# Feature sums in place on VectorE, the embedding's products behind the early pairs, and the gated embedding joined to the residual early

## The chip, the cores and the metric

The kernel runs on one core of a Trainium2 chip. It is one launch of some 43,600 instructions over five engines: TensorE (PE in the rows: matmuls, and PEld for its weight loads), VectorE (DVE), ScalarE (ACT), GpSimd (POOL) and SyncE (SP), which only issues DMAs. The metric is the device time in microseconds (us). Each engine runs its own list of instructions in the order in which the program laid it down, and waits on semaphores for the others.

## The reference

Two transformer-like blocks on a sequence of 1024 tokens with 1024 features. The change lies at the end of the second block, after its four branches have been merged:

```python
h = _layer_norm(DEEPNORM_ALPHA * h + merged @ w_out[i], ln1_g[i], ln1_b[i])
ffn = jnp.square(jax.nn.relu(h @ mlp_w1[i])) @ mlp_w2[i]
ple = jax.nn.sigmoid(h @ ple_gate_w[i]) * (p[i] @ ple_w[i])
h = _layer_norm(DEEPNORM_ALPHA * h + ffn + ple, ln2_g[i], ln2_b[i])
```

`mlp_w1` is 1024 x 4096, `mlp_w2` 4096 x 1024, `ple_gate_w` 1024 x 1024 and `ple_w` 256 x 1024. `p` is an input of 1024 x 256. All are fp32.

## The kernel before, in words

Activations lie transposed: 8 tiles of 128 features by 1024 tokens, in two chunks of 512 tokens. Each fp32 operand is split into a high part (a cast on ScalarE, L130 or L152) and a low part (a subtraction on VectorE, L131, or on GpSimd, L154), and a product is three matmuls: high by high, low by high, high by low (`mm3`, L160 to L162).

**The end of the second block** has these stages. The out-projection (`wo2`) makes one chunk of `h` after the other into 8 tiles `hs` (names `r` in the rows); a generator, `layer_norm`, is stepped between the matmuls and normalizes one chunk while the next is projected. Its sums over features are GpSimd additions (L2323), then one small matmul group for the mean (L2292), a spread of it by transposes (L2298), squares on ScalarE (L2333) that are added on GpSimd and VectorE in turn (L2335), a second pair L2292 and L2298, and the scaling (L2346, L2347). `done` splits the finished tiles into `hx`. Then come the embedding `p @ ple_w` (L2030 to L2053; 96 matmuls; result `wd`, "embedding", in DRAM), the products with `mlp_w1` and `ple_gate_w`, and the products with `mlp_w2`.

**The class `Seven`.** `h @ w` for a pair of 128-column groups of weights and the two chunks of tokens is a 2 x 2 block product. It is made with seven block products in place of eight (Winograd's form). A block product is 4 tiles x 3 = 12 matmuls of 512 columns. The features' sums t1 to t4 (differences of quarters of `h`) are made once, by `differences`; the weights' sums s1 to s4 are made per pair on GpSimd by `prepare` (L2204 to L2212), split, and consumed by `run`. There are 20 pairs: 16 of `mlp_w1` (`squared`), 4 of `ple_gate` (`gated`). The first two products of a pair, w11 y11 and w12 y21, need only plain quarters of `h` from the first chunk; for the first four pairs (EARLY) they are made ahead of the others, by `first`, while the second chunk is still being normalized. The `finish` functions square or gate a result and store it to DRAM. The gated result ("gated") and `h` itself ("normed") are read back ahead of the `mlp_w2` stage and joined to the residual.

**What sets the order.** The Tile framework places the instructions on the engines' lists by the order in the code and by when buffers come free, and adds the waits. Buffers come from rings of one SBUF pool: 29 slots, 11 temps, 6 weight buffers (`w`), 2 side buffers for loads (`l`), and 8 PSUM banks. SP issues nearly all DMAs from one list, in order: a DMA that waits for its data or its buffer holds up all DMAs behind it.

## Time and profile before

| what | us |
|---|---|
| three runs: lowest, median, highest | 3174.11, 3179.6, 3182.74 |
| the profiled execution, device time | 3182.6 |
| its span in the profile | 3180.8 |
| TensorE busy in it | 3038.2 |
| VectorE, ScalarE, GpSimd busy in it | 1785.6, 1151.4, 648.9 |

Times in the rows are us from the span's start. In a row of the timeline stand start, duration, engine, line, operation, output<-inputs, shape and count, and in brackets how long the engine was idle before it and what released it. The matmuls overlap, so a matmul's own duration (0.39) is longer than the distance to the next one's start (0.23). The out-projection of the second chunk ends at 2314, the embedding stands from there to 2353, the early pairs to 2379, the runs of the 20 pairs from 2404 to 2780, and the `mlp_w2` stage from there to the end.

### The profile page before, as it was taken

The numbers are of one execution on the slowest core, as the hardware profiler recorded it, in microseconds if no ns is written. First come the engines' busy times: TensorE is split into PE (matmuls) and PEld (weight loads), VectorE is DVE, ScalarE is ACT, GpSimd is POOL, SyncE is SP. The second block draws the span as 40 slices with busy tenths as digits, with TensorE's granted clock in tenths as the row PEclk, the third lists the DMA queues.
The fourth block names the chain that finished last, engine by engine and source line by source line (L and its number), as shares of the span: only waits on it lengthen the run. The fifth ranks groups of instructions, "written<-read, shape, count | busy, mean of one in ns | idle before, by whom it ended". The sixth has DMA issues, their size and how long they took to land.

```text
span 3180.8 us, 43621 instructions
## 1 busy us (share of the span) xinstructions
PE 3038.2 (96%) x17300; PEld 2647.7 (83%) x17300; DVE 1785.6 (56%) x3207; ACT 1151.4 (36%) x2192; POOL 648.9 (20%) x377
## 2 busy tenths in 40 slices
PE   8999999999999999999999998899977999989998
PEld 7999999999999778878877787687755888868887
DVE  4626777562567555354374647746657777652324
ACT  4224663222456442232245545512342222321113
POOL 1222001122200321010001000036624333212211
PEclk9999999999999999999999999999998999999999
DMA  3210004322000411111221010354242333562311
GB/s 119 81 65 25 16 21 165 113 68 83 27 11 27 152 63 57 57 49 54 86 94 67 34 40 30 105 184 140 92 178 83 119 111 109 194 225 91 96 60 54
DMA packets 111196, 273.94 MB, mean 86 GB/s; under 512 B 21372, under 2 KB 28540, under 8 KB 110992
## 3 DMA queue, kind: packets, MB, share of 16 engines
q1 hardware_dynamic: 109504, 266.52, 24.5%
q0 software_dynamic: 1488, 4.64, 0.6%
q8 instruction: 136, 2.23, 0.3%
q14 instruction: 68, 0.56, 0.1%
HBM read 202.79 MB, written 68.32 MB: 85 GB/s over the span
## 4 chain that ended last, share of the span: by engine, by line
PE 81%; DVE 8%; ACT 5%; DMA 2%; issue 2%; POOL 1%; SPq 0%; ACTq 0%; DVEq 0%; POOLq 0%
PE pj L160 13%; PE pj L162 13%; PE pj L161 13%; PE z L162 4%; PE z L161 4%; PE z L160 4%; PE fg L160 3%; PE fg L162 3%; PE fg L161 3%; PE pt L595 2%; PE x L1353 1%; PE sc L160 1%; PE sc L161 1%; PE sc L162 1%; PE sc L554 1%
## 5 line engine op out<-in xcount | busy, mean ns | idle before, releaser
L160 PE MATMUL pj<-hh,wih 128*128 128x348 f32 x864 | 278.8, 328 | 10.0 <-ACT wih L152 6.3
L161 PE MATMUL pj<-hl,wih 128*128 128x348 f32 x864 | 281.4, 326 | 3.4 <-DVE hl L690 3.2
L162 PE MATMUL pj<-hh,wil 128*128 128x348 f32 x864 | 280.0, 325 | 1.4 <-POOL wil L154 1.4
L160 PE MATMUL pj<-gh,m2h 128*128 128x512 f32 (+1 forms) x560 | 211.6, 378 | 12.3 <-ACT m2h L152 12.3
L160 PE MATMUL fg<-xx,fw 128*128 128x512 f32 x512 | 215.3, 421 | 0.0
L162 PE MATMUL pj<-gh,m2l 128*128 128x512 f32 (+1 forms) x560 | 210.4, 376 | 0.5 <-POOL m2l L154 0.5
L161 PE MATMUL pj<-gl,m2h 128*128 128x512 f32 (+1 forms) x560 | 210.1, 375 | 0.0
L162 PE MATMUL fg<-xx,fw 128*128 128x512 f32 x512 | 205.1, 401 | 0.4 <-DVE fw L131 0.4
L161 PE MATMUL fg<-xx,fw 128*128 128x512 f32 x512 | 204.8, 400 | 0.0
L2139 DVE TENSOR_TENSOR r<-pj,r 128x512 f32<-128x512 f32 (+1 forms) x104 | 67.3, 648 | 196.4 <-PE pj L162 196.2
L160 PEld LDWEIGHTS pj<-hh,wih 128*128 128x128 f32 x864 | 164.2, 191 | 11.8 <-ACT wih L152 6.3
L726 DVE TENSOR_TENSOR u<-pj,r 128x348 f32<-128x348 f32 x108 | 54.2, 518 | 211.1 <-PE pj L162 202.4
L161 PEld LDWEIGHTS pj<-hl,wih 128*128 128x128 f32 x864 | 165.2, 191 | 4.9 <-DVE hl L690 4.9
L162 PEld LDWEIGHTS pj<-hh,wil 128*128 128x128 f32 x864 | 164.9, 191 | 1.7 <-POOL wil L154 1.7
L131 DVE TENSOR_TENSOR ptl<-pt,pth 116x348 fp32r<-116x348 f32 (+2 forms) x268 | 150.4, 586 | 20.3 <-ACT pth L130 16.2
L130 ACT CAST pth<-pt 116x348 fp32r<-116x348 f32 (+2 forms) x268 | 128.4, 513 | 79.9 <-PE pt L595 70.6
L154 POOL TENSOR_TENSOR wil<-wi,wih 128x1024 fp32r<-128x1024 f32 x34 | 84.4, 2483 | 322.9 <-PE pj L161 302.3
L160 PEld LDWEIGHTS pj<-gh,m2h 128*128 128x128 f32 x560 | 105.6, 189 | 33.3 <-ACT m2h L152 12.7
L555 DVE TENSOR_REDUCE mx<-sc 116x1 f32<-116x348 f32 (+3 forms) x204 | 105.0, 514 | 40.3 <-PE sc L554 37.5
L154 POOL TENSOR_TENSOR wol<-wo,woh 128x1024 fp32r<-128x1024 f32 x24 | 58.1, 2421 | 329.1 <-PE pj L161 209.5
L562 ACT ACTIVATE p<-sc,mx 116x348 f32<-116x348 f32 (+3 forms) x204 | 109.6, 548 | 41.9 <-DVE mx L558 40.4
L162 PEld LDWEIGHTS pj<-gh,m2l 128*128 128x128 f32 x560 | 105.4, 188 | 21.5 <-POOL m2l L154 1.2
(687 smaller groups left out, 8601.7 us busy)
## 6 DMA issues: line engine op xcount, KB each, us to landing
wo<-in_w_out_dram SPq DMA_DIRECT2D x39, 512.0 KB, 3.4
x<-in_mlp_w_dram SPq DMA_DIRECT2D x36, 512.0 KB, 3.6
wi<-in_w_in_dram SPq DMA_DIRECT2D x34, 512.0 KB, 3.5
fr<-in_w_in_dram SPq DMA_DIRECT2D x64, 256.0 KB, 2.8
gates<-fg SPq DMA_DIRECT2D x64, 256.0 KB, 2.0
gs<-gates SPq DMA_DIRECT2D x32, 512.0 KB, 4.1
squares<-ge SPq DMA_DIRECT2D x64, 256.0 KB, 2.3
g<-squares SPq DMA_DIRECT2D x32, 512.0 KB, 3.6
```

Source lines behind the costliest of these rows:

```text
L130: nc.scalar.copy(hi, src)
L131: nc.vector.tensor_tensor(lo, src, hi.bitcast(F32), ALU.subtract)
L154: eng.tensor_tensor(lo[:, o], raw[:, o], hi[:, o].bitcast(F32), ALU.subtract)
L160: mm(out, a[0], b[0], start=start, stop=False)
L161: mm(out, a[0], b[1], start=False, stop=False)
L162: mm(out, a[1], b[0], start=False, stop=stop)
L554: nc.tensor.matmul(o, q2[:, qs], krl[:, ks], start=False, stop=True)
L555: nc.vector.tensor_reduce(mx[:n, x : x + 1], o, AX.X, ALU.max)
L562: nc.scalar.activation(p[:n, ks], o, AF.Exp, bias=mx[:n, 3:4], accum_out=mx[:n, 4 + x : 5 + x])
L595: nc.tensor.transpose(pt[:KT, x : x + n], p[:n, kt * KT : (kt + 1) * KT], c.ident[:n, :n])
L726: nc.vector.tensor_tensor(t[:, lo : lo + n], ps, r[:, lo : lo + n], ALU.mult)
L2139: nc.vector.tensor_tensor(t[:, o], ps, t[:, o], ALU.add)
```

## The change

- `differences` makes all sums on VectorE, in place in the `r` tiles, kind by kind (t3, t2, t1, t4), where before VectorE and GpSimd shared them tile by tile, with temps `td`.
- `run` takes its products in another order, s4 (with the plain quarter y22) first, and makes its sums in place; there is one more addition in a pair, since the product of s2 is added into two results. `prepare` makes all four sums before its first pause and splits s4 first.
- The embedding's loads, splits and products stand behind the four early pairs, which have the preparation of pair 0 behind them.
- `normed` is stored by `done`, in 16 halves as each is ready, where before 8 whole tiles were stored after `differences`.
- `squared` and `gated` finish in place in the result tiles. `gated` also loads `normed` and joins it (ALPHA h + gated embedding) before its store, so the 8 loads of `normed` and the 8 joins ahead of the `mlp_w2` stage are gone, and the 8 loads of `gated` stand in that stage's first loop.

```diff
@@ -1989,11 +1989,13 @@
     hs = [c.temp("r1") for f in range(8)]
+    hd = c.dr.tile([8, P, 1024], F32, name="normed")
...
         def done(f, o):
+            nc.sync.dma_start(out=hd[f][:, o], in_=hs[f][:, o])
             if f >= 4 or o.start == 0:
                 c.split(*hx[f].at(o.start, o.stop - o.start), hs[f][:, o])
@@ -2025,54 +2027,29 @@
-    hd = c.dr.tile([8, P, 1024], F32, name="normed")
-    px = []
-    for k in range(2):
-        t = c.load("p", a["p"][k])
-        px.append(c.split_new("p", t, 1024))
-    wp = []
...
-    for f in range(8):
-        s = c.temp("pw")
...
-        c.proj(wp[f], px, TCHUNK, evac)
-        next(old, None)
-        nc.sync.dma_start(out=wd[f], in_=s[:, T])
...
     def squared(p):
-        def finish(i, j, src):
-            b = c.temp("ge")
-            q = b[:, 512:1024]
-            nc.vector.scalar_tensor_tensor(q, src, 0.0, src, ALU.max, ALU.mult)
-            nc.sync.dma_start(out=fd[2 * p + i][:, j * 512 : j * 512 + 512], in_=q)
+        def finish(i, j, z):
+            nc.vector.scalar_tensor_tensor(z, z, 0.0, z, ALU.max, ALU.mult)
+            nc.sync.dma_start(out=fd[2 * p + i][:, j * 512 : j * 512 + 512], in_=z)
...
     def gated(p):
-        def finish(i, j, src):
+        def finish(i, j, z):
             b = c.temp("ge")
             o = slice(j * 512, j * 512 + 512)
-            nc.sync.dma_start(out=b[:, 0:512], in_=wd[2 * p + i][:, o])
-            q = b[:, 512:1024]
-            nc.scalar.activation(q, src, AF.Sigmoid)
-            nc.vector.tensor_tensor(q, q, b[:, 0:512], ALU.mult)
-            nc.sync.dma_start(out=pd[2 * p + i][:, o], in_=q)
+            e, h = b[:, 0:512], b[:, 512:1024]
+            nc.sync.dma_start(out=e, in_=wd[2 * p + i][:, o])
+            nc.sync.dma_start(out=h, in_=hd[2 * p + i][:, o])
+            nc.scalar.activation(z, z, AF.Sigmoid)
+            nc.vector.tensor_tensor(z, z, e, ALU.mult)
+            nc.vector.scalar_tensor_tensor(h, h, ALPHA, z, ALU.mult, ALU.add)
+            nc.sync.dma_start(out=pd[2 * p + i][:, o], in_=h)
@@ -2081,15 +2058,37 @@
         for w in work[:EARLY]:
             w.first(y, lambda: next(old, None))
+        prep = work[0].prepare()
+        next(prep)
+
+        px = []
+        for k in range(2):
+            t = c.load("p", a["p"][k])
+            px.append(c.split_new("p", t, 1024))
...
+        for f in range(8):
+            s = c.slot("pw")
...
+            c.proj(wp[f], px, TCHUNK, evac)
+            next(old, None)
+            nc.sync.dma_start(out=wd[f], in_=s[:, T])
...
         y.update(differences(c, hs))
-        for f in range(8):
-            nc.sync.dma_start(out=hd[f], in_=hs[f][:, T])
         del hs
-        prep = work[0].prepare()
         for _ in prep:
             pass
@@ -2106,14 +2105,6 @@
-        if f0 == 0:
-            for f in range(8):
-                t, s = c.temp("r2"), c.slot("r2")
-                nc.sync.dma_start(out=t[:, T], in_=hd[f])
-                nc.sync.dma_start(out=s[:, T], in_=pd[f])
-                nc.vector.scalar_tensor_tensor(t[:, T], t[:, T], ALPHA, s[:, T], ALU.mult, ALU.add)
-                hs.append(t)
-            del t, s
@@ -2132,6 +2123,9 @@
             for f in range(8):
+                if f0 == 0:
+                    hs.append(c.temp("r2"))
+                    nc.sync.dma_start(out=hs[f][:, T], in_=pd[f])
                 t = hs[f]
@@ -2182,13 +2176,14 @@
-        z = c.temp("za")[:, 0:512]
+        z = self.new("za")[:, 0:512]
@@ -2207,10 +2202,10 @@
+        add(s4, x12, s2, ALU.subtract)
+        add(s3, x11, x21, ALU.subtract)
         yield
-        add(s3, x11, x21, ALU.subtract)
-        add(s4, x12, s2, ALU.subtract)
-        for name, src in (("s2", s2), ("s3", s3), ("s1", s1), ("22", x22), ("s4", s4)):
+        for name, src in (("s4", s4), ("s3", s3), ("s2", s2), ("s1", s1), ("22", x22)):
@@ -2229,48 +2224,52 @@
-        add(u2, self.p1, self.product(w.pop("s2"), take("t2")))
+        u, v = c.temp("zu"), c.temp("zv")
+        z12, z21, z22 = u[:, 0:512], u[:, 512:1024], v[:, 0:512]
+        add(z12, self.p1, self.product(w.pop("s4"), take("22")))
         along()
-        add(u3, u2, self.product(w.pop("s3"), take("t3")))
+        add(z21, self.p1, self.product(w.pop("s3"), take("t3")))
+        along()
+        p6 = self.product(w.pop("s2"), take("t2"))
+        add(z21, z21, p6)
+        add(z12, z12, p6)
         along()
         p5 = self.product(w.pop("s1"), take("t1"))
-        add(z[:, 0:512], u3, p5)
-        add(u2, u2, p5)
-        self.finish(1, 1, z[:, 0:512])
+        add(z22, z21, p5)
+        add(z12, z12, p5)
+        self.finish(1, 1, z22)
+        self.finish(0, 1, z12)
         along()
-        add(u3, u3, self.product(w.pop("22"), take("t4")))
-        self.finish(1, 0, u3)
-        along()
-        add(z[:, 512:1024], u2, self.product(w.pop("s4"), take("22")))
-        self.finish(0, 1, z[:, 512:1024])
+        add(z21, z21, self.product(w.pop("22"), take("t4")))
+        self.finish(1, 0, z21)
         along()
 def differences(c, hs):
...
-    for j in range(4):
-        s = c.temp("td")
-        x, y = hs[j], hs[j + 4]
-        nc.vector.tensor_tensor(s[:, 0:512], x[:, 512:1024], x[:, 0:512], ALU.subtract)
-        nc.vector.tensor_tensor(s[:, 512:1024], y[:, 512:1024], s[:, 0:512], ALU.subtract)
-        put("t2", s[:, 512:1024])
-        put("t1", s[:, 0:512])
-        r = c.temp("td")
-        nc.gpsimd.tensor_tensor(r[:, 0:512], y[:, 512:1024], x[:, 512:1024], ALU.subtract)
-        nc.gpsimd.tensor_tensor(r[:, 512:1024], y[:, 0:512], s[:, 512:1024], ALU.subtract)
-        put("t3", r[:, 0:512])
-        put("t4", r[:, 512:1024])
+    out = {"t3": [], "t2": []}
+    for j in range(4):
+        add(y11[j], y12[j], y11[j], ALU.subtract)
+    for j in range(4):
+        add(y12[j], y22[j], y12[j], ALU.subtract)
+        out["t3"].append(put("t3", y12[j]))
+    for j in range(4):
+        add(y22[j], y22[j], y11[j], ALU.subtract)
+        out["t2"].append(put("t2", y22[j]))
+    out["t1"] = [put("t1", y11[j]) for j in range(4)]
+    for j in range(4):
+        add(y21[j], y21[j], y22[j], ALU.subtract)
+    out["t4"] = [put("t4", y21[j]) for j in range(4)]
     return out
```

Three places show how the instructions stand. A bracket lists the engines and DMA lanes that a row waits for.

**SP between the out-projection and the runs**, before: `p` are the two input tiles, `wp` the two weight tiles of the embedding, `x` weights of pairs (L151 for early pairs, L2199 for `prepare`). A side buffer holds each `p`, and the next `x` of L2199 (pair 0's) takes it over.

```order
L151 DMA x_3354_21236<-in_mlp_w_dram 128x1024 [waits DMAHW6_49,PE_49,Pool_49]
L151 DMA x_3364_21291<-in_mlp_w_dram 128x1024 [waits DMAHW7_49,PE_49,Pool_49]
L108 DMA p_21031<-in_p_dram 128x1024 [waits DVE_49,PE_49]
L108 DMA p_21037<-in_p_dram 128x1024 [waits PE_49]
L151 DMA x_3372_21342<-in_mlp_w_dram 128x1024 [waits DMAHW0_49,Pool_49]
L2199 DMA x_3412_21508<-in_mlp_w_dram 128x1024 [waits DMAHW6_49,DMAHW1_49,DVE_49]
L2040 DMA wp_21043<-in_ple_w_dram 128x1024 [waits DMAHW2_49]
L2199 DMA x_3413_21509<-in_mlp_w_dram 128x1024 [waits DMAHW7_49,DMAHW3_49,DVE_49]
L2040 DMA wp_21049<-in_ple_w_dram 128x1024 [waits DMAHW4_49]
L2053 DMA embedding<-pw_21055 128x1024 [waits DMAHW5_49,Activation_49]
```

Now the same place, with the last load of an early pair (L151), the second load of pair 0 and both of pair 1 (L2194: `x_3347`, then `x_3412` and `x_3413`) and the stores of early results (L2038):

```order
L2194 DMA x_3347_21229<-in_mlp_w_dram 128x1024 [waits DMAHW0_49]
L151 DMA x_3339_21190<-in_mlp_w_dram 128x1024 [waits DMAHW1_49,PE_49,Pool_49]
L2038 DMA squares<-za_21076 128x512 [waits DMAHW2_49,DVE_49]
L108 DMA p_21238<-in_p_dram 128x1024 [waits DMAHW6_49,DMAHW3_49,Pool_49]
L2038 DMA squares<-za_21130 128x512 [waits DMAHW4_49,DVE_49]
L2038 DMA squares<-za_21180 128x512 [waits DMAHW5_49,DVE_49]
L108 DMA p_21244<-in_p_dram 128x1024 [waits DMAHW0_49,DVE_49]
L2038 DMA squares<-za_21224 128x512 [waits DMAHW7_49,DVE_49]
L2194 DMA x_3412_21545<-in_mlp_w_dram 128x1024 [waits DMAHW3_49,DVE_49]
L2071 DMA wp_21250<-in_ple_w_dram 128x1024 [waits DMAHW1_49]
L2194 DMA x_3413_21546<-in_mlp_w_dram 128x1024 [waits DMAHW6_49,DMAHW2_49,DVE_49]
L2071 DMA wp_21256<-in_ple_w_dram 128x1024
```

The loads of `p`, the `x` that take over their buffers and the `wp` stand in the same order among themselves as before, but behind all loads of the early pairs and pair 0, and in between the early pairs' stores.

**VectorE ahead of the embedding**, before: the last evacuations of the out-projection (L2008), and the low parts of `p` and `wp`.

```order
L2008 SCALAR_TENSOR_TENSOR r_3246_20411<-xx_11665,r_3246_20411 128x512 [waits DVE_49]
L2008 SCALAR_TENSOR_TENSOR r_3247_20412<-xx_11669,pj_20999 128x512 [waits PE_49]
L2008 SCALAR_TENSOR_TENSOR r_3247_20412<-xx_11669,r_3247_20412 128x512 [waits DVE_49]
L131 TENSOR_TENSOR pl_21034<-p_21031,ph_21033 128x1024 [waits DMAHW6_49,Activation_49]
L131 TENSOR_TENSOR pl_21040<-p_21037,ph_21039 128x1024 [waits DMAHW7_49,Activation_49]
L131 TENSOR_TENSOR wpl_21045<-wp_21043,wph_21044 128x1024 [waits DMAHW2_49,Activation_49]
L131 TENSOR_TENSOR wpl_21051<-wp_21049,wph_21050 128x1024 [waits DMAHW4_49,Activation_49]
```

Now, from the last addition of the normalization's squares (L2334) on, with sums and squares of the early pairs (`za`, L2180, L2037) and the low parts of pair 0's five weights (`xs`, `xx`):

```order
L2334 TENSOR_TENSOR ln_20715<-ln_20715,ln_20716 128x512 [waits Activation_49,Pool_49]
L2037 SCALAR_TENSOR_TENSOR za_21180<-za_21180 128x512 [waits DVE_49]
L131 TENSOR_TENSOR xs_21514<-sb_21233,xs_21514 128x512 [waits DMAHW6_49,DMAHW4_49,DMAHW2_49]
L131 TENSOR_TENSOR xs_21517<-sb_21233,xs_21517 128x512 [waits DMAHW3_49,DMAHW1_49]
L131 TENSOR_TENSOR xs_21520<-sa_21232,xs_21520 128x512 [waits DMAHW7_49,DMAHW5_49,Activation_49]
L131 TENSOR_TENSOR xs_21523<-sa_21232,xs_21523 128x512 [waits DMAHW3_49,Activation_49]
L131 TENSOR_TENSOR xx_21526<-x_3347_21229,xx_21526 128x512 [waits DMAHW0_49,Activation_49]
L2180 TENSOR_TENSOR za_21224<-z_21211,p_3343_21209 128x512 [waits PE_49]
L2037 SCALAR_TENSOR_TENSOR za_21224<-za_21224 128x512 [waits DVE_49]
L131 TENSOR_TENSOR pl_21241<-p_21238,ph_21240 128x1024 [waits DMAHW3_49,Activation_49]
L131 TENSOR_TENSOR pl_21247<-p_21244,ph_21246 128x1024 [waits DMAHW6_49,Activation_49]
L131 TENSOR_TENSOR wpl_21252<-wp_21250,wph_21251 128x1024 [waits DMAHW1_49,Activation_49]
```

The low parts of `p` and `wp` now stand behind the squares' sums of the normalization, behind pair 0's splits, and behind the last early pair's result.

**SP at the start of the `mlp_w2` stage**, before: `m` are its weights in order of use (the third of them here), `r` the loads ahead of it.

```order
L2113 DMA r_3924_24314<-gated 128x1024 [waits DMAHW1_49,PE_49]
L2112 DMA r_3925_24318<-normed 128x1024 [waits DMAHW2_49]
L2113 DMA r_3926_24319<-gated 128x1024 [waits DMAHW3_49,PE_49]
L2112 DMA r_3927_24323<-normed 128x1024 [waits DMAHW4_49]
L2113 DMA r_3928_24324<-gated 128x1024 [waits DMAHW5_49,PE_49]
L2112 DMA r_3929_24328<-normed 128x1024 [waits DMAHW6_49,PE_49]
L2113 DMA r_3930_24329<-gated 128x1024 [waits DMAHW7_49]
L2112 DMA r_3931_24333<-normed 128x1024 [waits DMAHW0_49,Activation_49]
L2113 DMA r_3932_24334<-gated 128x1024 [waits DMAHW1_49]
L2112 DMA r_3933_24338<-normed 128x1024 [waits DMAHW2_49,Activation_49]
L2113 DMA r_3934_24339<-gated 128x1024 [waits DMAHW3_49]
L151 DMA m_3945_24423<-in_mlp_w_dram 128x640 [waits DMAHW4_49,Pool_49]
```

Now, from the second weight on; `ge` are the loads of the last pair's finish:

```order
L151 DMA m_3854_24335<-in_mlp_w_dram 128x640 [waits DMAHW7_49,Pool_49]
L108 DMA g_24285<-squares 128x1024 [waits DMAHW2_49,DVE_49]
L2052 DMA gated<-ge_24158 128x512 [waits DMAHW1_49,DVE_49]
L108 DMA g_24627<-squares 128x1024 [waits DMAHW6_49,DVE_49]
L151 DMA m_3860_24377<-in_mlp_w_dram 128x640 [waits DMAHW7_49,DMAHW3_49,Pool_49]
L2047 DMA ge_24225<-embedding 128x512 [waits DMAHW4_49]
L2048 DMA ge_24225<-normed 128x512 [waits DMAHW5_49]
L2047 DMA ge_24232<-embedding 128x512 [waits PE_49]
L2048 DMA ge_24232<-normed 128x512
L2047 DMA ge_24253<-embedding 128x512 [waits DMASW7_49,DMAHW0_49,DMASW5_49,PE_49]
L2048 DMA ge_24253<-normed 128x512 [waits DMAHW1_49]
L2128 DMA r_3847_24291<-gated 128x1024 [waits DMAHW2_49,DMASW1_49]
```

The third weight stood behind all 16 loads of `normed` and `gated`; now it stands ahead of the last six loads of the finish and of the first load of `gated`.

## Rows read from the trace of the kernel before

**Rows 1.** Waits of TensorE, 2220 to 2840: total, times, longest.

```profile
PE z L160 <- ACT xs L130: 25.2, 1, 25.2
PE pj L160 <- ACT m2h L152: 12.3, 1, 12.3
PE pj L160 <- ACT wph L130: 12.0, 1, 12.0
PE z L162 <- DVE xs L131: 5.3, 1, 5.3
```

**Rows 2.** Stretches: us, busy times (counts), granted clock, DMA share, GB/s.

```profile
2360.00:2410.00 50.00, 18.98 (x76) 13.92 (x74) 44.71 (x46) 21.32 (x37) 26.56 (x16) 0.73 0.36 137
2410.00:2700.00 290.00, 288.88 (x1237) 233.33 (x1238) 205.28 (x262) 67.63 (x106) 96.34 (x63) 0.99 0.32 109
2775.00:2830.00 55.00, 42.29 (x175) 33.39 (x174) 30.85 (x33) 15.09 (x18) 8.61 (x6) 0.88 0.82 301
```

**Rows 3.** Chain that ended last, out-projection to embedding: start, us, what.

```profile
2317.45 1.05 ACT ph L130
2318.53 1.76 DVE pl L131
2320.31 0.33 SPq L2199
2320.69 4.54 DMA wp<-in_ple_w_dram
2325.30 1.05 ACT wph L130
2326.40 0.79 PE pj L160
```

**Rows 4.** Timeline of TensorE: early pairs' start, runs' start.

```profile
2353.00 0.39 PE L160 MATMUL z<-xx,x1h 128*128 128x512 f32 x1
2353.23 0.39 PE L161 MATMUL z<-xx,x1h 128*128 128x512 f32 x1
...
2411.12 0.79 PE L162 MATMUL z<-t,xs 128*128 128x512 f32 x1 [5.35 <-DVE xs L131]
2411.71 0.63 PE L160 MATMUL z<-t,xs 128*128 128x512 f32 x1
2412.14 0.63 PE L161 MATMUL z<-t,xs 128*128 128x512 f32 x1
```

**Rows 5.** Timeline of VectorE, differences, and the second pair's first sum.

```profile
2384.91 11.30 DVE L131 TENSOR_TENSOR t<-td,t 128x512 fp32r<-128x512 f32 x8
...
2419.51 0.69 DVE L131 TENSOR_TENSOR xs<-sb,xs 128x512 fp32r<-128x512 f32 x1
...
2428.84 0.69 DVE L2228 TENSOR_TENSOR zu<-z,p 128x512 f32<-128x512 f32 x1 [0.76 <-PE z L162]
```

**Rows 6.** Timeline of VectorE, embedding stage and later low parts.

```profile
2326.38 1.22 DVE L131 TENSOR_TENSOR wpl<-wp,wph 128x1024 fp32r<-128x1024 f32 x1 [4.96 <-ACT wph L130]
...
2339.36 2.48 DVE L2331 TENSOR_TENSOR r<-r,lb 128x512 f32<-128x512 f32 x4 [6.80 <-PE lb L2298]
```

**Rows 7.** Timeline of GpSimd: early weights, differences, weights' sums.

```profile
2317.94 1.26 POOL L2323 TENSOR_TENSOR ln<-ln,r 128x512 f32<-128x512 f32 x1 [0.69 <-DVE r L2008]
...
2359.47 2.42 POOL L154 TENSOR_TENSOR x1l<-x,x1h 128x1024 fp32r<-128x1024 f32 x1 [11.12 <-PE z L161]
...
2386.07 1.71 POOL L2271 TENSOR_TENSOR td<-r,td 128x512 f32<-128x512 f32 x1
...
2431.87 1.29 POOL L2204 TENSOR_TENSOR sa<-x 128x512 f32<-128x512 f32 x1 [17.98 <-DMA x<-in_mlp_w_dram]
```

**Rows 8.** Timeline of TensorE around the third `mlp_w2` weight.

```profile
2793.81 0.40 PE L162 MATMUL pj<-gh,m2l 128*128 128x512 f32 x1
2806.46 0.79 PE L160 MATMUL pj<-gh,m2h 128*128 128x512 f32 x1 [12.25 <-ACT m2h L152]
...
2810.01 0.45 PE L160 MATMUL pj<-gh,m2h 128*128 128x512 f32 x1
```

**Rows 9.** Chain that ended last ahead of that weight.

```profile
2786.97 8.99 DMA r<-normed
2796.02 9.58 DMA m<-in_mlp_w_dram
2805.68 0.73 ACT m2h L152
```

More of the change, by code (lines that the diff above doesn't have):

```diff
@@ L2083, in second_half, with evac @@
             w.first(y, lambda: next(old, None))
+        prep = work[0].prepare()
[4 more added lines that the diff above has]
+            px.append(c.split_new("p", t, 1024))
+        wp = []
+        for i in range(2):
+            raw, hi, lo = c.slot("wp"), c.slot("wph", F32R), c.slot("wpl", F32R)
+            nc.sync.dma_start(out=raw[:, T].rearrange("p (k m) -> p k m", m=P), in_=a["ple_w"][i])
+            c.split(hi[:, T], lo[:, T], raw[:, T])
+            for f in range(4):
+                wp.append([x[:, f * 256 : f * 256 + 256].rearrange("p (k m) -> p k m", k=2) for x in (hi, lo)])
+        del raw, hi, lo
+        for f in range(8):
+            s = c.slot("pw")
+            def evac(i, lo, m, ps):
+                nc.scalar.copy(s[:, lo : lo + m], ps)
+            c.proj(wp[f], px, TCHUNK, evac)
+            next(old, None)
+            nc.sync.dma_start(out=wd[f], in_=s[:, T])
+        del px, wp, s
         for _ in old:
@@ L2165, in __init__ @@
         self.c, self.w1, self.w2, self.finish = c, w1, w2, finish
-        self.w, self.p1 = {}, None
+        self.w, self.p1, self.new = {}, None, c.temp
     def product(self, w, y):
@@ L2191, in first @@
         w = [x.rearrange("p k m -> p (k m)") for x in self.c.weight("x1", self.w1)]
+        self.new = self.c.slot
         self.both([x[:, 0:512] for x in w], [x[:, 512:1024] for x in w], y["11"], y["21"], along)
@@ L2252, in differences @@
 def differences(c, hs):
-    nc = c.nc
-    out = {n: [] for n in ("t1", "t2", "t3", "t4")}
+    add = c.nc.vector.tensor_tensor
+    y11, y12 = [t[:, 0:512] for t in hs[:4]], [t[:, 512:1024] for t in hs[:4]]
+    y21, y22 = [t[:, 0:512] for t in hs[4:]], [t[:, 512:1024] for t in hs[4:]]
     def put(n, src):
```

14 lines of the change are left out of this document (1 added, 13 removed).

## The prediction

> **What bounds the kernel now.** I read the page's busy shares first: TensorE works 3038.2 of 3180.8 us, so the whole question is where its remaining idle time lies in the stages that the change touches. TensorE's waits from 2220 to 2840 name three places [rows 1]: 12.0 us ahead of the embedding (for the cast of `wp`), 25.2 and 5.3 us ahead of the runs (for pair 0's weights), and 12.3 us in the `mlp_w2` stage (for its third weight). The stretches show that nothing else is to be had there: from 2410 to 2700 TensorE is busy 288.9 of 290 us, with VectorE at 205 and GpSimd at 96 [rows 2]. The chain of waits then tells why each place is late.
>
> Ahead of the embedding the chain goes from the cast and the low part of `p` to an SP issue that could go only then, to the `wp` load behind it, and to the cast of `wp` [rows 3]. From the end of the low part (2318.53 + 1.76 = 2320.29) to the first matmul (2326.40) it is 6.1 us. Ahead of the runs the end is VectorE making low parts of the differences [rows 5]. In the `mlp_w2` stage the weight's load was issued at 2796.0, behind the loads of `normed` and `gated`, and took 9.6 us [rows 9].
>
> **The embedding behind the early pairs.** At 2314.2, where before TensorE stood idle, the early pairs can start: their first two weights are loaded and split without needing the embedding. They are 8 products of 12 matmuls at 0.2325 us (the distance of two starts [rows 4]), 22.3 us, and some 1.2 for the normalization's small matmuls between them: they end at 2337.8. Nothing is saved by the swap itself; it saves only if the embedding's inputs are there by then.
>
> They aren't, by the order. `wp` is still issued behind an `x` load that takes the buffer of `p`, thus after the low part of `p`, and on VectorE that low part now stands behind the sum of the last early pair. So it can't begin before 2337.8 + 0.7 + 0.7, takes 1.2 [rows 6], and with the 6.1 us of the chain the embedding can't begin before 2346.5. VectorE is later still. The early pairs' two first sets of matmuls and the mean end at 2323.9; the squares' sums then wait for a GpSimd addition that now stands behind the low part of the third early weight (from 2319.8, the end of the first pair, 2.4), pair 0's four sums (1.3 to 1.7 each, I take 6.0) and the fourth early weight (2.4), and takes 1.3 itself [rows 7]: 2331.9. VectorE goes on with an addition and a square (1.4), four subtractions (2.5 [rows 6]), an addition (0.7), the wait for one more GpSimd addition (1.3), and an addition and a square (1.4): 2339.2. Five low parts at 0.6 (0.69 alone, [rows 5]), with one wait for a cast between them (in all 3.1), the last pair's sum and square (1.3) and the low part of `p` (1.2): 2344.8. Plus 6.1: the embedding begins at 2351. I take this one, with 2346.5 below it and 2355 above it (GpSimd's operations all at 1.7 and a `wp` load 2 us longer).
>
> The embedding took 2326.40 to 2353.00 with its slow first matmuls [rows 3, 4], 26.6 us, and takes the same behind an idle time of like length: it ends at 2377.6.
>
> **The differences.** They begin when the second chunk is normalized. Its second spread now comes after two of the embedding's eight features, about 10 us into it; VectorE's scaling of 8 tiles takes 5.3 us, and ScalarE follows, in between the evacuations of the embedding. So first sums start at some 16 us of 26.6, and the plain quarter y22 is split by 22. The first product of pair 0, now s4 with y22, finds all it needs at 2377.6 (pair 0's weights were split ahead of the embedding) and covers 2.8 us. VectorE needs 4 + 4 + 4 subtractions and 2 more, then four low parts for t3: at 0.6 to 0.7 us that ends at about 29 us, 2380, when the second product is due at 2380.4. t2 follows 2.5 us later against a product of 2.8 us, t1 and t4 likewise. So no wait beyond 1 us, if VectorE runs at its short duration. Before, its low parts there took 11.30 / 8 = 1.41 us against 0.69 alone [rows 5], with GpSimd computing differences beside them at 1.71 [rows 7]; the order now has no GpSimd instruction there, since pair 1's sums stand earlier and pair 2's wait for a load that goes after the first run.
>
> What the profile shows of this is that two-operand VectorE instructions stretch while GpSimd computes, and sums with a PSUM operand (0.69) don't. The Trainium skill's page "SBUF — State Buffer", section "Who interferes with whom", says that a VectorE instruction with two SBUF inputs contends with a GpSimd one that reads SBUF for an exclusive lock, and that one with a single SBUF input doesn't. The rows agree (1.41 against 0.69 us). By this rule the in-place squares, with both inputs in SBUF, are exposed wherever GpSimd's sums fall on them; rival D is what that would do here at its worst.
>
> Pair 0's run began in effect at 2411.1, with slow matmuls. Its end is the second pair's first sum less a product, 2428.84 - 2.8 = 2426.05 [rows 5]. Now it is 2377.6 + 60 x 0.2325 = 2391.5. **Gain 34.5 us.** The bounds of the embedding's start make it 30.5 to 39.
>
> **The runs.** VectorE gets one more addition of 0.69 us per pair, 20 in all, and 16 joins; it is busy 205 of 290 us, so this lies beside the matmuls. In a run of five products (13.9 us) the first product now needs s4, GpSimd's fourth sum in place of its third. After the second operand of the next pair is free, 2.7 us into a run, come a load (3.4), four sums (5.2 at 1.29), a cast and a low part (1.3): 12.6 of 13.9. That is close; I take 1 us lost in all for the two runs concerned, 0 to 6 as bounds (a load that takes 3 us longer, twice). Longer runs have two products more that need no sum. `normed` stored in halves puts 8 issues ahead of the first early load, which has to be there at 2309 only: by the scaling's end it goes some 1.4 us later than before and is hidden by GpSimd.
>
> **The `mlp_w2` stage.** From 2793.81 to 2810.01 eight steps at 0.2325 (1.9) stood in 16.2 us [rows 8]: 14.3 us lost, with the slow matmuls. Now the third weight is issued ahead of the last pair's six loads, once GpSimd has split the second, 3 us before the runs end. It is needed 14 us after. The fourth stands behind four loads of `gated` (2 MB), which at the stretch's 301 GB/s [rows 2] are 7 us, and is needed 21 us after. So the wait goes: **gain 14.3 us**, 0 as the bound below, since the finish now issues 6 loads and 3 stores in those same us.
>
> **The sum.** 34.5 + 14.3 - 1 = 47.8. From the profiled execution's 3182.6 us that is 3134.8; it is 3.0 us above the median of the runs shown, so 3132 us against 3179.6.
>
> **The rivals.** A, the forecast: 3132, own range 3124 to 3141. Chance 0.66.
>
> B, the wait ahead of the embedding goes altogether. Then another 13.2 us and the slow start of 3 us are won: 3116. The order of SP and VectorE speaks against it; for it, that the chain is short if VectorE isn't late. Chance 0.09.
>
> C, a wait takes the place of the one removed: the wait in the `mlp_w2` stage stays, since the last finish's loads and `gated` share the DMA queue with the weights (+12 to 14), or the t3 low parts come late because ScalarE's casts for them stand behind the embedding's evacuations (up to four casts and low parts late, 6 us), or the early runs' sums are late (+6). One of them gives 3138 to 3146, two 3150. Chance 0.17.
>
> D, slower: VectorE becomes the bound of the runs. If every instruction of it with two SBUF operands took the long duration, a long run would have 4 in-place squares and 5 low parts at 1.75, a low part of twice the width at 2.1 and 8 sums at 0.65, 23 us against 19.5 of matmuls, and an early run 18.8 against 13.9: 16 x 3.5 + 4 x 4.9 = 76 us more, 3208. It decides if GpSimd's sums cover some two thirds of a run or more. They are busy 96 of 290 us [rows 2], and the change gives GpSimd nothing there. Chance 0.04.
>
> E, the change only moves the waits: the differences are no earlier than the embedding's end plus their own 30 us. 3175 to 3182. The splits of the second chunk in the midst of the embedding speak against it. Chance 0.04.
>
> **How the numbers follow.** Faster by over 0.3% (9.5 us, about what a measurement of this kernel can tell): A, B, C and part of E, 0.92. Within 0.3%: 0.03. Slower: D and mishaps like it, 0.05. The range is A's with B's time at its foot and two waits of C at its head: 3116 to 3150.
>
> **What would show it.** In the new profile TensorE's waits should list about 13 us ahead of the embedding, for the cast of `wp`, now at about 2338 to 2351; next to nothing for t3 or `xs` behind it; pair 0's run from about 2378; and no 12 us at the third `mlp_w2` weight. VectorE's low parts of t should take 0.7 us. If the embedding starts at 2338, B holds; if TensorE waits for t or for an `m2` cast, C; if it waits between the runs' products for `xs`, D.

## The result and the profile after

The changed kernel takes 3144.0 us (median of 4 runs, 3139.9 to 3146.1) against 3179.6: 0.9888 of the time before, 95% interval 0.987 to 0.9906. That is 35.6 us faster; 47.8 were forecast, and 3132 lay 12 us below the measured time. The profiled execution has a span of 3140.5 us (3180.8 before).

TensorE's waits between 2220 and 2840 (engine, line and what it waited for; total, times, longest), which answer to [rows 1]:

```profile
PE pj L160 <- ACT wph L130: 14.4, 1, 14.4
PE z L160 <- ACT xs L130: 3.2, 2, 1.6
PE pj L161 <- DVE gl L131: 2.1, 2, 1.3
PE pj L160 <- ACT m2h L152: 1.4, 1, 1.4
...
PE pj L162 <- POOL m2l L154: 0.9, 1, 0.9
```

The 25.2 and 5.3 us ahead of the runs are gone, and so is the 12.3 us one. The wait ahead of the embedding stays, as forecast. New are short waits in two places: for `xs` (3.2 in two), and for the squares' low parts and a weight in the `mlp_w2` stage (4.4 in four).

The chain that ended last (start, us, what) shows both the old wait and the first of the new ones; its head answers to [rows 3]:

```profile
2339.23 1.23 DVE pl L131
2340.86 5.70 DMA wp<-in_ple_w_dram
2346.58 1.05 ACT wph L130
2347.68 0.80 PE pj L160
...
2378.43 0.69 DVE t L131
2379.20 6.49 POOL sb L2206
2385.68 1.26 POOL sa L2200
2387.01 1.28 POOL sb L2205
2388.31 0.63 ACT xs L130
```

Up to the first matmul this is the chain of the forecast: `p`'s low part, the `wp` load issued behind it, the cast. Then comes something that the forecast didn't have: one of GpSimd's four sums for pair 1's weights takes 6.49 us, the two behind it 1.26 and 1.28, and the cast for run 1's first weight comes after them.

**Where to measure.** The profiled executions differ already ahead of the change: the output projection's last matmul ends at 2314.4 before and at 2309.6 after, and between 2307.8 and 2317.2 in the kernels below. A difference of spans carries that along. So stages are compared from there. Timeline of TensorE, the last matmuls of the output projection and of the 20 pairs, after:

```profile
2309.24 0.40 PE L162 MATMUL pj<-mgh,wo2l 128*128 128x512 f32 x1
...
2746.73 0.40 PE L162 MATMUL z<-t,xx 128*128 128x512 f32 x1
```

From these two ends: 437.5 us up to the runs' end, and 393.4 from there to the span's end. The same two, in us:

| kernel | to the runs' end | from there to the end | both | against the changed kernel |
|---|---|---|---|---|
| before | 465.9 | 400.5 | 866.4 | +35.5 |
| changed | 437.5 | 393.4 | 830.9 | 0 |
| old differences (u_diff) | 443.0 | 391.0 | 834.0 | +3.1 |
| embedding back (u_move) | 450.3 | 390.4 | 840.7 | +9.8 |
| old join (u_join) | 437.3 | 396.7 | 834.0 | +3.1 |
| pair 0's weights late (u_prep) | 438.1 | 392.3 | 830.4 | -0.5 |
| old product order (u_order) | 435.5 | 392.6 | 828.1 | -2.8 |
| inputs early (inputs) | 423.4 | 392.6 | 816.0 | -14.9 |
| pair 1's sums early (sums) | 434.2 | 392.6 | 826.8 | -4.1 |
| two sums on VectorE (vsums) | 435.6 | 393.4 | 829.0 | -1.9 |
| gate pairs earlier (gmid) | 437.1 | 386.6 | 823.7 | -7.2 |
| combination 1 (all4) | 424.2 | 389.5 | 813.7 | -17.2 |
| combination 2 (best2) | 424.2 | 389.8 | 814.0 | -16.9 |
| combination 3 (best3) | 421.7 | 385.6 | 807.4 | -23.5 |

The table is of one profiled execution of each kernel. Two kernels whose edits lie behind the runs or late in them (u_join, gmid) come within 0.4 us of the changed kernel up to the runs' end. From there to the end six kernels whose edits lie ahead (u_diff, u_move, u_prep, inputs, sums, vsums) take 390.4 to 393.4, so a difference under 3 us there says nothing by itself. In part it is the clock: in u_diff (391.0) and u_move (390.4) TensorE's granted clock stays at 1.00 in this stage, in the changed kernel it is 0.50 from 2774.75 to 2778.10.

The change's 35.5 us agree with the 35.6 of the medians. Pair 0's run ends at 2387.3 after, 77.7 us behind the output projection's end, and at 2426.05 before, 111.6 behind it: 33.9 won there. From that end to the runs' end the kernel now takes 359.8 us instead of 354.3, 5.6 lost; the rest of the program is 7.1 shorter.

Timeline of TensorE at the starts of runs 1 and 2, and two of the slow matmuls of run 2, after:

```profile
2387.05 0.40 PE L162 MATMUL z<-t,xx 128*128 128x512 f32 x1
2388.98 0.50 PE L160 MATMUL z<-xx,xs 128*128 128x512 f32 x1 [1.53 <-ACT xs L130]
...
2402.88 0.40 PE L162 MATMUL z<-t,xx 128*128 128x512 f32 x1
2404.91 0.50 PE L160 MATMUL z<-xx,xs 128*128 128x512 f32 x1 [1.63 <-ACT xs L130]
...
2407.15 0.63 PE L160 MATMUL z<-xx,xs 128*128 128x512 f32 x1
...
2409.28 0.50 PE L162 MATMUL z<-xx,xs 128*128 128x512 f32 x1
```

The two waits are 3.2 of the 5.6 us; most of the others are slow matmuls behind the second. Timeline of VectorE there, after (compare [rows 5]):

```profile
2374.81 6.11 DVE L131 TENSOR_TENSOR t<-r,t 128x512 fp32r<-128x512 f32 x10 [0.24 <-ACT t L130]
2380.84 1.28 DVE L2271 TENSOR_TENSOR r<-r 128x512 f32<-128x512 f32 x2
2382.05 2.49 DVE L131 TENSOR_TENSOR t<-r,t 128x512 fp32r<-128x512 f32 x4
```

The low parts take 0.61 us each, not 1.41, and TensorE waits for none of them. GpSimd's 6.49 us lie beside them: they end at 2385.69, 1.15 us after the last low part (2384.54).

SP's issues around the end of the runs, after:

```profile
2751.99 0.33 SPq L151 DMA_DIRECT2D m<-in_mlp_w_dram  x1
2752.38 0.42 SPq L2047 DMA_DIRECT2D ge<-embedding  x1
...
2754.75 0.55 SPq L2048 DMA_DIRECT2D ge<-normed  x1
2755.40 0.39 SPq L2128 DMA_DIRECT2D r<-gated  x1
2761.49 2.25 SPq L2052 DMA_DIRECT2D gated<-ge  x3
2763.79 1.39 SPq L2128 DMA_DIRECT2D r<-gated  x3
2765.28 0.38 SPq L151 DMA_DIRECT2D m<-in_mlp_w_dram  x1
```

The third weight now goes ahead of the last finish's six loads, as forecast, and TensorE doesn't wait for it. But SP then stands from 2755.8 to 2761.5 at that finish's stores, whose data wait for these loads, and the fourth weight goes behind them at 2765.28.

### The profile page after: what moved, and what is told of

The parts are those of the page before. It is cut to its first block, busy times and chain, and to the rows that moved or that the text cites. A ratio compares the mean times of both kernels' runs of the same rounds, so it can differ in the third digit from the quotient of the medians.

```text
span 3140.5 us, 43671 instructions
## 1 busy us (share of the span) xinstructions
PE 3032.8 (97%) x17300; PEld 2642.9 (84%) x17300; DVE 1750.8 (56%) x3243; ACT 1145.8 (36%) x2192; POOL 625.5 (20%) x369
## 4 chain that ended last, share of the span: by engine, by line
PE 79%; DVE 9%; ACT 6%; DMA 2%; issue 2%; POOL 2%; SPq 0%; ACTq 0%; DVEq 0%; POOLq 0%
PE pj L162 13%; PE pj L160 13%; PE pj L161 13%; PE z L160 4%; PE z L162 4%; PE z L161 4%; PE fg L160 3%; PE fg L162 3%; PE fg L161 3%; PE pt L595 2%; PE x L1353 1%; PE po L161 1%; PE po L160 1%; PE po L162 1%; PE sc L160 1%
## 5 line engine op out<-in xcount | busy, mean ns | idle before, releaser
L161 PEld LDWEIGHTS pj<-gl,m2h 128*128 128x128 f32 x560 | 105.5, 188 | 23.3 <-DVE gl L131 2.7
```

The costliest lines, as they stand in the source:

```text
L161: mm(out, a[0], b[1], start=False, stop=False)
```

## The experiments

Two theories for the missing 12 us, and their rivals. Early runs: pair 1's sums are late by a tile and by standing beside VectorE; or run 1's loads and casts are late by themselves. `mlp_w2` stage: the last finish's loads hold SP and the queue; or the 4 MB of `gated` do. Beside these: what each part of the change is worth, and whether the embedding's 14.4 us are only the order of buffers and issues. Ratios are to the kernel before, with 95% intervals.

**u_diff: the old differences in the changed kernel.** `differences` is that of before, its second half on GpSimd.

```diff
-    for j in range(4):
-        add(y11[j], y12[j], y11[j], ALU.subtract)
...
+        nc.gpsimd.tensor_tensor(r[:, 0:512], y[:, 512:1024], x[:, 512:1024], ALU.subtract)
+        nc.gpsimd.tensor_tensor(r[:, 512:1024], y[:, 0:512], s[:, 512:1024], ALU.subtract)
```

> The changed kernel (3144.0) with the differences of the kernel before: row by row over j, half of them on GpSimd, in tiles of their own. Theory: they are what lets pair 0's run begin. Begun at 2362 like the new ones, 8 subtractions at 0.7 to 1.6, four low parts of y22 and 15 low parts at 1.0 to 1.4 put the last t3 at 2389 to 2395, where the second product needs it at 2376: +12 to +20 us, 3156 to 3164. Rival: kind by kind matters, GpSimd beside VectorE doesn't: 15 low parts at 0.61 end at 2379, +3 to +4 us, 3148.

3149.9 us, 0.9902 (0.9886 to 0.9917); up to the runs' end +5.5 us. Neither number: 5.9 us above the changed kernel, between the rival's 3 to 4 and the theory's 12 to 20. The durations are nearer the theory's. Timeline of VectorE, the 16 low parts:

```profile
2384.07 15.19 DVE L131 TENSOR_TENSOR t<-td,t 128x512 fp32r<-128x512 f32 x16
```

Timeline of GpSimd, two of pair 1's sums beside them:

```profile
2388.47 1.53 POOL L2199 TENSOR_TENSOR sa<-x 128x512 f32<-128x512 f32 x1 [3.20 <-ACT t L130]
2389.96 1.75 POOL L2206 TENSOR_TENSOR sb<-x,x 128x512 f32<-128x512 f32 x1
```

The low parts beside GpSimd's sums, apart from the others (group of VectorE from 2389.0 to 2395.5: count, busy us, mean ns):

```profile
L131 DVE TENSOR_TENSOR t<-td,t 128x512 fp32r<-128x512 f32 x4 | 6.9, 1782 | 0.0
```

So the 0.95 us that a low part takes on average are a mixture: 1.75 to 1.80 us beside GpSimd (five of the 16), 0.68 without it. What I had missed is that a product takes its four tiles one after the other: TensorE ran its second and third products at VectorE's pace, with waits for `t` of 4.5 us in all, instead of standing until the last t3. And the early runs' starts wait less here (0.6 us for `xs` in two).

**u_move: the embedding back ahead of the early pairs.**

```diff
+        px = []
+        for k in range(2):
+            t = c.load("p", a["p"][k])
...
         for w in work[:EARLY]:
             w.first(y, lambda: next(old, None))
         prep = work[0].prepare()
         next(prep)
-        px = []
-        for k in range(2):
-            t = c.load("p", a["p"][k])
...
```

> The changed kernel with the embedding back ahead of the early pairs. Theory: the move is worth something only through the differences, which then begin some 14 us later against the matmuls (at about 2376, when the early pairs end at 2371), so TensorE waits for t3 about 10 to 12 us; the early runs' starts lose less: +7 to +14 us, 3151 to 3158. Rival: the whole gain of 34 us is the differences' own, the move gives nothing: 3141 to 3147.

3155.1 us, 0.9921 (0.9909 to 0.9934), 11.1 us above the changed kernel and +9.8 in the stages: the theory. TensorE waits for `t` 9.2 us in six places. GpSimd there has the clearest case of the stretch. Its timeline:

```profile
2387.55 9.49 POOL L2199 TENSOR_TENSOR sa<-x 128x512 f32<-128x512 f32 x1 [14.27 <-DVE t L131]
2397.00 1.29 POOL L2206 TENSOR_TENSOR sb<-x,x 128x512 f32<-128x512 f32 x1
```

VectorE's timeline in the same microseconds:

```profile
2391.00 2.49 DVE L131 TENSOR_TENSOR t<-r,t 128x512 fp32r<-128x512 f32 x4
2393.40 1.29 DVE L131 TENSOR_TENSOR xs<-sb,xs 128x512 fp32r<-128x512 f32 x2
2394.61 1.29 DVE L131 TENSOR_TENSOR xs<-sa,xs 128x512 fp32r<-128x512 f32 x2
```

One sum takes 9.49 us and ends at 2397.04, 1.14 after VectorE's train (2395.90); the next takes 1.29.

**u_join: the residual joined as before.**

```diff
-            nc.vector.scalar_tensor_tensor(h, h, ALPHA, z, ALU.mult, ALU.add)
-            nc.sync.dma_start(out=pd[2 * p + i][:, o], in_=h)
+            nc.sync.dma_start(out=pd[2 * p + i][:, o], in_=z)
...
+        if f0 == 0:
+            for f in range(8):
...
+                nc.vector.scalar_tensor_tensor(t[:, T], t[:, T], ALPHA, s[:, T], ALU.mult, ALU.add)
```

> The changed kernel with the residual joined as before: the finish loads no normed, and ahead of mlp_w2's first chunk 16 loads and 8 VectorE instructions make ALPHA * normed + gated. Theory: the join gave 7 us, the difference of the stretch from the runs' end to the program's end (400.6 to 393.5): 3151, with a wait of about 12 us for the third weight, and no short waits for the squares' low parts. Rival: the extra loads of the last pair's finish cost what the early join gives: 3142 to 3146.

3145.9 us, 0.9892 (0.9879 to 0.9906). TensorE's waits from 2720 to 2840:

```profile
PE pj L160 <- ACT m2h L152: 8.2, 1, 8.2
PE pj L162 <- POOL m2l L154: 0.4, 1, 0.4
```

The third weight's wait is back, but with 8.2 us, not 12.3, and the stretch is 3.3 us longer; the median, 1.9 us above the changed kernel, is the rival's. The stretch is longer than in any kernel with the join (at most 393.4), so the join is worth 3 to 6 us there by the spread named above. The rest of that stage's 7.1 comes with other parts of the change, which is not taken apart further here.

**u_prep: pair 0's weights asked for behind the differences.**

```diff
-        prep = work[0].prepare()
-        next(prep)
...
         del hs
+        prep = work[0].prepare()
         for _ in prep:
```

> The changed kernel with pair 0's weights (loads, sums, splits) asked for behind the differences again, as before the change. Theory: the wait ahead of the embedding is made by these two loads, which take both side buffers at the output projection's end; without them p is loaded at once, the embedding starts at 2333 to 2338, and pair 0's weights are still ready by its end, since nothing else uses GpSimd there: 3128 to 3135. Rival: pair 0's splits, asked for last, stand behind the differences on ScalarE and VectorE as before the change, TensorE waits for xs ahead of run 0, which eats the gain: 3142 to 3155.

3144.4 us, 0.9892 (0.9875 to 0.9908): no gain, the rival's number, though half of the theory holds. SP's issues:

```profile
2312.70 0.33 SPq L108 DMA_DIRECT2D p<-in_p_dram  x1
...
2321.65 16.85 SPq L2038 DMA_DIRECT2D squares<-za  x4
2338.55 0.42 SPq L2068 DMA_DIRECT2D wp<-in_ple_w_dram  x1
```

`p` is loaded at once, and the wait ahead of the embedding falls from 14.4 to 7.4 us; what is left is `wp` behind the stores of the early squares. The 7 us are given back at run 0: TensorE waits 2.4 us for `t` and 1.9 for `xs`, and the starts of three more runs lose 0.7 to 0.9 each; slow matmuls follow the waits of run 0.

**u_order: the products in the order of before.**

```diff
-        add(z12, self.p1, self.product(w.pop("s4"), take("22")))
-        add(z21, self.p1, self.product(w.pop("s3"), take("t3")))
...
+        add(u2, self.p1, self.product(w.pop("s2"), take("t2")))
+        add(u3, u2, self.product(w.pop("s3"), take("t3")))
```

> The changed kernel with the products of a pair in the order of before (s2, s3, s1, x22, s4; the sums in two tiles, the squares still in place). Theory: s4 with the plain quarter y22 first is what covers the first low parts of the differences: without it run 0 waits for t2 (made behind t3) 4 to 7 us with its slow matmuls; the starts of runs 1 and 2, whose s2 needs only two of the four sums, win back 2 to 5: 3144 to 3148. Rival: the order is worth nothing at run 0, only the early starts gain: 3139 to 3141.

3140.7 us, 0.9882 (0.9867 to 0.9897), -2.8 us in the stages: the rival's number, but half of the theory's mechanism. Run 0 waits 2.4 us for `t`, and no early run's start waits, although GpSimd's sum is as late and as long as in the changed kernel. Its timeline:

```profile
2381.32 6.49 POOL L2205 TENSOR_TENSOR sb<-x,x 128x512 f32<-128x512 f32 x1 [24.40 <-DVE t L131]
```

With its wait and the slow matmuls behind it run 0 ends 81.4 us behind the output projection's end, where it ended 77.7 behind it in the changed kernel. That covers the sums in any order: the last of the four, that of s4, is done 78.4 behind it. At run 2's start both kernels stand 95.3 us behind the output projection's end. So up to there the two orders are worth the same here; nearly all of the 2.0 us by which this one is shorter up to the runs' end are run 2's slow matmuls (1.8 us), which it doesn't have.

**inputs: the embedding's inputs early.** `p` and `ple_w` are loaded into slots, issued after the first early pair, and split after the second and third.

```diff
+            if n == 0:
+                for k in range(2):
+                    raws.append(c.slot("p"))
+                    nc.sync.dma_start(out=raws[k][:, T], in_=a["p"][k])
...
+            if n == 1:
+                px = [c.split_new("p", raws.pop(0), 1024) for k in range(2)]
```

> The changed kernel with the loads of p and ple_w in slots instead of side buffers, issued as soon as the output projection frees slots, their casts and low parts after the second and third early pair. Theory: the 14.4 us ahead of the embedding are only the chain of buffer, SP issue and load; the second normalization's later steps are tied to the embedding's features and move with it: the embedding starts at about 2333, 3126 to 3130. Rival: VectorE's backlog sets the start of pair 0's run, the wait goes to the products with y22 and t3: 3138 to 3144.

3133.5 us, 0.9851 (0.9837 to 0.9866), 10.5 us below the changed kernel, and -14.9 us in the stages. The profiled execution was the fastest of the four (3125.5; the others 3130.7 to 3136.8), so the gain is 10 to 15 us. The median lies between the two forecasts; the mechanism is the theory's. TensorE waits nowhere for `wph`, and the normalization, the differences and run 0 move along with the embedding. Two waits of 2.5 us in all at the fourth early weight are new: its load went behind those of `p` and `wp`.

**sums: pair 1's sums asked for before run 0 takes its two tiles.**

```diff
             after = work[n + 1].prepare() if n + 1 < len(work) else iter(())
+            if n == 0:
+                next(after)
             w.run(y, lambda: next(after, None), n + 1 == len(work))
```

> The changed kernel with pair 1's weight sums asked for before run 0 takes its two tiles zu and zv, so that they get the first free tiles. In the changed kernel the sum into sb could start only at 2379.20, when VectorE's low parts freed a tile, then stood 6.49 us beside them, and the starts of runs 1 and 2 lost 5.6 us with their slow matmuls. Theory: the late tile and the stretch beside VectorE's train are what makes these starts late. Now the four sums end near 2360 at 1.3 us each, neither start waits: 3138 to 3140. Rival: pair 1's loads or casts hold the starts by themselves, or zu is now late in its turn: 3143 to 3146.

3142.6 us, 0.9876 (0.9861 to 0.9891), which is above the theory's range and within 0.4 us of the rival's; the stages say -4.1, of which -3.3 in the runs. Timeline of GpSimd, with pair 1's last two sums and pair 2's first:

```profile
2354.74 1.28 POOL L2207 TENSOR_TENSOR sb<-x,sa 128x512 f32<-128x512 f32 x1 [2.50 <-PE ls L2293]
2355.98 1.29 POOL L2208 TENSOR_TENSOR sb<-x,x 128x512 f32<-128x512 f32 x1
2396.91 1.30 POOL L2201 TENSOR_TENSOR sa<-x 128x512 f32<-128x512 f32 x1 [39.64 <-DMA x<-in_mlp_w_dram]
```

The stretched sum is gone and run 1 starts without a wait, run 2 with 0.2 us; run 3 now waits 1.2 us. The medians alone (1.4 us) would not have told this from nothing.

**vsums: two of pair 1's sums on VectorE, the tile as late as it was.** Between "late tile" and "beside VectorE" the run before doesn't choose; this one does.

```diff
-            after = work[n + 1].prepare() if n + 1 < len(work) else iter(())
+            after = work[n + 1].prepare(nc.vector if n == 0 else None) if n + 1 < len(work) else iter(())
...
+        add = (eng or nc.gpsimd).tensor_tensor
         add(s4, x12, s2, ALU.subtract)
         add(s3, x11, x21, ALU.subtract)
```

> The changed kernel with two of pair 1's four sums (s3, s4) on VectorE behind its low parts; their tile stays as late as it was. Theory: GpSimd's 6.49 us is time in which it waits beside VectorE's train of low parts; without it VectorE has both sums at about 2386 and the cast at about 2387, run 1 starts 0.5 us late or less instead of 1.5. Rival: the late tile alone makes run 1 late, the start is where it was. Either is under 3 us: 3141 to 3145, to be read in the trace.

3143.2 us, 0.9884 (0.987 to 0.9897), as both forecasts said; the trace decides. Timeline of VectorE:

```profile
2386.98 2.49 DVE L131 TENSOR_TENSOR t<-r,t 128x512 fp32r<-128x512 f32 x4
2389.39 0.69 DVE L2224 TENSOR_TENSOR zu<-z,p 128x512 f32<-128x512 f32 x1
2389.99 0.69 DVE L2207 TENSOR_TENSOR sb<-x,x 128x512 f32<-128x512 f32 x1
2390.59 0.69 DVE L2206 TENSOR_TENSOR sb<-x,sa 128x512 f32<-128x512 f32 x1
```

Run 1 starts at 2392.22, 0.23 us behind the last matmul of run 0: no wait. So the late tile alone doesn't make run 1 late, as the rival had it; GpSimd's 6.49 us beside VectorE do, with the sums that stand behind them. One of those, s2, isn't behind them here (GpSimd makes it at 2359.80), so the run doesn't part the 6.49 us from their queue. Run 2 still waits, 2.7 us here: that one comes from the loads, which the pair ahead lets go late.

**gmid: the gate pairs ahead of the last four pairs of squares.**

```diff
-        work = [squared(p) for p in range(16)] + [gated(p) for p in range(4)]
+        work = [squared(p) for p in range(12)] + [gated(p) for p in range(4)] + [squared(p) for p in range(12, 16)]
```

> The changed kernel with the four gate pairs ahead of the last four pairs of squares, so that the last finish loads nothing (its six loads of embedding and normed are gone from the mlp_w2 stage, its three stores stay). There the changed kernel loses 7 us: the squares' low parts come 0.8 and 1.3 us late, the fourth weight 1.4 and its low part 0.9, and the matmuls behind them are slow. Theory: the last pair's loads take the queue and SP: all four waits go, 3136 to 3138. Rival: the eight loads of gated (4 MB) ahead of the fourth weight hold it, whatever the finish does: its wait stays, 2 us or less are won, 3142 to 3145.

3138.9 us, 0.9871 (0.9855 to 0.9887); -6.8 us from the runs' end on, and 0.4 ahead of it. TensorE's waits from 2720 to 2840, all of them:

```profile
PE pj L162 <- POOL m2l L154: 0.6, 1, 0.6
```

The theory's mechanism, 0.9 us above its range: without the last finish's loads the weights and squares are in time, with all of `gated` loaded there as before. Of the 6.8 us the waits are 3.8 (4.4 to 0.6); the clock no longer falls in this stage either.

**The combinations.** all4 is inputs + sums + gmid, with each `mlp_w2` weight asked for ahead of its tile of `gated`. best2 leaves that last edit out and asks for `p` and `ple_w` ahead of the early pairs. best3 is best2 with x22 split third:

```diff
-        for name, src in (("s4", s4), ("s3", s3), ("s2", s2), ("s1", s1), ("22", x22)):
+        for name, src in (("s4", s4), ("s3", s3), ("22", x22), ("s2", s2), ("s1", s1)):
```

> The inputs of the embedding early, pair 1's sums early, the gate pairs ahead of the last squares, and each mlp_w2 weight asked for before the tile of gated that its feature adds to. Theory: the gains add, since they lie in three stages one after the other: 14.9 us (the stages' time in the profile of the kernel with early inputs), 5 and 7: 3117 to 3120. Rival: the embedding's earlier start has used up VectorE's slack, so early sums on GpSimd and t3 collide: 3125 to 3130.

> Inputs of the embedding loaded ahead of the early pairs in the program's order (so that their loads no longer stand behind a store of squares and push the fourth early weight back), pair 1's sums early, the gate pairs ahead of the last squares; the mlp_w2 weights are asked for as in the changed kernel. Theory: the three stages give 17 (embedding at about 2333 and no 2.5 us in the early pairs), 4 and 7 us: 3115 to 3118. Rival: as in the last combination the second early run loses 3 us and more to late loads, VectorE's backlog takes another 3: 3121 to 3125.

> As the run before, with the plain quarter x22 split third instead of last, so that its buffer is free earlier and the next pair's load goes earlier (in the order it then goes ahead of the stores of run 0). Theory: the wait of 3.3 us at run 2's start goes, 3 to 4 us less than the run before. Rival: the start of run 2 is not the buffer's but VectorE's, no difference beyond 1 us.

all4 3126.4 us, 0.9826 (0.9811 to 0.9841); best2 3130.7, 0.9844 (0.9831 to 0.9857); best3 3124.6, 0.981 to 0.9837 around 0.9824. all4 fell into its rival's range; best2, slower than both of its forecasts, lies nearer to the rival's. In the stages both have 17 of the 26 us. all4 waits 3.3 us at run 2's start for late loads; both wait again in the `mlp_w2` stage (all4 1.5 us for a weight), although the finish loads nothing there. In best3 neither place waits, its one edit gives 6.6 us instead of 3 to 4, and the stages are 23.5 us shorter than in the changed kernel, near the sum of the three (26.2). best3 is faster than both kernels by every measure here: 3124.6 against 3144.0 and 3179.6. Why splitting x22 earlier also frees the `mlp_w2` stage (385.6 against 389.8) I have not taken apart.

## Why the prediction was right or wrong

**The bound and the early pairs: right.** The early pairs take 23.8 us (forecast 23.5), with no wait.

**The wait ahead of the embedding: right, mechanism and size.** The embedding begins 38.0 us after the output projection's end, forecast 36.8 with bounds of 32.3 to 40.8. VectorE reached `p`'s low part 29.6 us after that end, forecast 29.4; from the low part's end the load took 5.70 us where [rows 3] had 4.54. The runs "inputs" and "u_prep" show that buffers and SP's order make it. Rival B's price, 16 us, lies just above the 10 to 15 that "inputs" won; with the order as it stood B didn't happen.

**The differences: the result right (gain 33.9 us, forecast 34.5), one reason wrong.** The low parts take 0.61 us and no product waits, but not because no GpSimd instruction lies beside them. One does; this time GpSimd was the one that took longer. That was luck: in u_diff the low parts beside GpSimd took 1.78 us each, where 0.68 is usual. The row by which the forecast showed that sums with a PSUM operand don't stretch (0.69 at 2428.84 [rows 5]) stands beside an idle GpSimd [rows 7]; the trace of before has a better one, 0.69 us at 2431.63 beside GpSimd's sum from 2431.87. And the gain isn't any one part's: up to the runs' end the old differences cost 5.5 us back, the old place of the embedding 12.8, against 28.4 that the whole change won there. The other 10 us come back with no single part undone; two parts undone together were not run.

**The early runs: the step that failed.** "Pair 1's sums stand earlier" was read from the order. The first did run early (at 2353.53), but the second needed a tile which VectorE freed only at 2379.20, and then stood beside its low parts for 6.49 us. Forecast 1 us lost, bounds 0 to 6; measured 5.6. Besides the waits of 3.2 us the clock took part: it fell behind the second wait, and the slow matmuls cost 1.8 us, a cost that the forecast's bounds (a late load, twice) didn't name. The forecast had noted that the first product now needs the fourth sum. That this made the lateness count is not shown: in u_order run 0 ended so late that the fourth sum would have been in time too.

**The `mlp_w2` stage: mechanism right, size half.** The third weight's wait went, as forecast; 7.1 us of 14.3 came. The sum's own caveat, six loads and three stores in the same microseconds, was the other half: gmid takes the loads away and gets 6.8 of the missing 7.2, though this stage spreads by 3 us from kernel to kernel. I had put it into the range and not into the sum.

**Rival D: no.** Windows of 250 us in the long runs, after (columns as [rows 2]):

```profile
2450.00:2700.00 250.00, 250.00 (x1078) 202.25 (x1077) 159.70 (x238) 58.86 (x96) 73.56 (x54) 1.00 0.36 120
```

VectorE is busy 159.7 of 250 us, the squares in place take 0.68, TensorE never waits.

The terms as measured, 33.9 - 5.6 + 7.1 = 35.4, give the 35.5 of the stages. The two mis-sized terms are the 12 us between forecast and result, and both are part of what rival C described. So the result, 3144.0, lies inside the stated range of 3116 to 3150, but above forecast A's own 3124 to 3141 (chance 0.66) and in the 3138 to 3146 that rival C gave for one such wait (chance 0.17). Rival E's 3175 to 3182 didn't come: pair 0's run ended 33.9 us earlier.

## What to carry to other kernels

An order of instructions says who goes first, not when: for each step that "stands earlier", look also for the tile that it writes and for whoever must free it. Where loads move into the last step of a stage, price the next stage's weights behind them in the queue, and put the step that needs no loads last instead. When a change has several parts that cover one wait, undo each alone before crediting one.

## What the runs showed of the hardware

GpSimd can lose to VectorE for a whole train: sums that take 1.29 us alone took 6.49 and 9.49 beside low parts of VectorE with two SBUF operands, ending 1.15 and 1.14 us after the last of these, while the low parts kept their 0.61 (from start to start; 0.68 each, since they overlap). Next to VectorE's sums with a PSUM operand GpSimd took 1.26 to 1.29. In u_diff both engines took longer instead, GpSimd 1.53 to 1.75 us a sum and VectorE 1.78 a low part beside them, in place of 0.68. The Trainium skill's page "SBUF — State Buffer", section "Who interferes with whom", says that two-input VectorE instructions contend with GpSimd's reads, and that issue order decides who blocks. All of these rows agree with the first. The second alone doesn't tell u_diff from the others, since there too GpSimd's first sum started inside VectorE's train; what does is open.

The clock answered like waits differently. Stretches around the starts of runs 1 and 2, after (columns as [rows 2]; the granted clock stands behind the five engines' busy times):

```profile
2388.00:2393.00 5.00, 4.02 (x17) 3.17 (x18) 4.04 (x7) 2.70 (x5) 0.28 (x1) 1.00 0.35 112
...
2404.90:2409.30 4.40, 4.39 (x12) 3.17 (x13) 4.40 (x8) 1.51 (x3) 0.00 (x0) 0.63 0.72 238
```

After 1.53 us of waiting the granted clock stayed at full speed (2.4 GHz). After 1.63 us, 16 us later, it was 0.63 on average over the next 4.4 us, mostly at the lower level of 1.2 GHz: eleven steps took 4.4 us instead of the 2.6 that they take at 0.2325 each. In vsums the same run's start waited longer, 2.69 us, and the clock stayed at full speed:

```profile
2408.90:2413.30 4.40, 4.26 (x18) 3.39 (x19) 4.28 (x8) 1.65 (x4) 0.00 (x0) 1.00 0.61 194
```

So the length of the wait alone doesn't tell whether the clock falls. What does is open.
